# Two zero-padded q tiles per head, taken from a ring shared with the retention's states

## The chip, the cores and the metric

The kernel runs on one core of a Trainium2 chip. The metric is the device time of one execution in microseconds (us). TensorE (PE) does the matrix products and the transposes, VectorE (DVE) and ScalarE (ACT) work on their results, GpSimd (POOL) splits weights and copies small tiles, and the queue of SyncE (SP) issues most of the transfers. Each engine works through its own list of instructions in order. An instruction that waits for another engine also holds up everything behind it in its own list.

## What is computed

Two layers of a decoder over 1024 positions of width 1024. The part that matters here is layer 0's group A (8 heads of 64, each query keeps its 256 best keys) and layer 1's group C (4 heads with two softmax maps each). Both form scores block by block, 128 queries at a time against all keys up to the block:

```python
def causal_attention(q, k, v, scale):
    ...
    def block(args):
        qb, i = args
        qpos = i * QBLK + jnp.arange(QBLK)
        s = jnp.einsum('bqhd,bkhd->bhqk', qb, k).astype(jnp.float32) * scale
        s = jnp.where((kpos[None, :] <= qpos[:, None])[None, None], s, -jnp.inf)
        p = jax.nn.softmax(s, axis=-1).astype(v.dtype)
        return jnp.einsum('bhqk,bkhd->bqhd', p, v)
```

Group A does the same with a mask of the kept keys. Group B of layer 0 is a retention: a state per head is carried from chunk to chunk, `state = g * state + k'v`. Group D of layer 1 is a latent attention, which the change does not touch.

## The kernel before

Products in full precision are made from values split in two: a high part, and a low part that holds the remainder. For a pair of heads of A, `qs[r]` (r = 0, 1) holds the head's high q in 64 partitions and its low q in the other 64. The scores of one block are therefore two products into `S` (function `scores`): `qs` with `kd` (the high keys twice, line 411), and the high q with `kl` (the low keys, line 412). For the second product the other half of the partitions must read zeros. So POOL copies the block's high q into a tile of 128x128 whose other half was zeroed at the start: `zq[r]`, one tile for each r, filled by `head_q` (line 417) and read by line 412. There are 192 such products, 96 in A and 96 in C, fed by 64 copies each.

Order. A heads' pair is a list of units. A unit of A takes one r and two neighbouring blocks q = 2j and 2j + 1, with j in the order 0, 3, 1, 2; so the two blocks of a unit use the same `zq[r]` one right after the other. A unit of C takes one block and both r. A pipeline (`pipe.run`) lets each unit's scores go ahead of the transposes (`tp`, line 309) of the unit before, and mixes in the projections of the next pair as filling. What stands where in each engine's list is decided when the program is built, by priorities and free buffers; the copies of `head_q` carry a high priority. On POOL the copies share the list with the splits of weights (line 251, `waqkl`, `wagl`, `wavl`, `wol`) and with those of the mixed rows (`mixl`).

Softmax: DVE reads `S`, adds the mask and takes the extreme (line 1024), ACT takes the exponential (line 1026), DVE scales the row (line 973). PE transposes the result into `tp`, from which DVE (line 995) or ACT (line 993) copies it to `pT`; `tp` has two buffers. The product with v goes to `bank`, is multiplied with the gate `gin` on DVE (line 1013) and stored by SP to `mixT` (line 1014).

Rings. `med` is a ring of 5 tiles of 1 KB per partition. From it come the retention's masked scores `bsT` and its states `bstate` (which use half of a tile), the gates `gin`, `dl` (line 1085), and the angles `ang` and `kk` of a rope table (lines 223 to 232, on DVE). Head pairs are named here pair 0 to pair 3.

Of the kernel before, what the change touches and what calls it, by code (L numbers as in the profile page):

```python
# [11 lines left out]
F32 = mybir.dt.float32  # L12
F32R = mybir.dt.float32r
# [8 lines left out]
P = 128  # L22
# [67 lines left out]
def chain(*gens):  # L90
    for g in gens:
        yield from g
# [53 lines left out]
def tile_hybrid_decoder(ctx: ExitStack, tc, x, positions, pre_norm, post_norm, w_in_even, w_out_even, w_in_odd,  # L146
# [4 lines left out]
    const = ctx.enter_context(tc.tile_pool(name="const", bufs=1))  # L151
# [5 lines left out]
    sm = ctx.enter_context(tc.tile_pool(name="sm", bufs=4))  # L157
# [4 lines left out]
    def nm(s):  # L162
        n_[0] += 1
        return f"{s}_{n_[0]}"
# [7 lines left out]
    def epg(s, shape=(P, T), dt=F32):  # L172
        return ep.tile(list(shape), dt, tag="e", name=nm(s))
# [5 lines left out]
        return sm.tile(list(shape), dt, tag=s, name=nm(s), bufs=bufs)  # L179

    def med(s, shape=(P, 256)):
        return sm.tile(list(shape), F32, tag="med", name=nm(s), bufs=5)

    def hf(s, shape=(P, 512)):
        return sm.tile(list(shape), F32, tag="hf", name=nm(s), bufs=2)
# [4 lines left out]
    V, A, G = nc.vector, nc.scalar, nc.gpsimd  # L190
# [20 lines left out]

    halfpi = const.tile([P, 1], F32, name="halfpi")
    V.memset(halfpi, math.pi / 2)

    zq = [const.tile([P, P], F32R, name=f"zq{r}") for r in range(2)]
    for r in range(2):
        V.memset(zq[r][64 - r * 64:128 - r * 64, :].bitcast(F32), 0.0)

    def rope_tables(half, at, tabs, pg=epg):

# [182 lines left out]
    def scores(S, qs, kd, kl, q, qz=None):  # L403
# [5 lines left out]
        for c in range(0, n, 512):  # L409
            w = min(512, n - c)  # L410
            nc.tensor.matmul(S[:, c:c + w], a, kd[:, c:c + w], start=True, stop=False)  # L411
            nc.tensor.matmul(S[:, c:c + w], b, kl[:, c:c + w], start=False, stop=True)  # L412

    def head_q(qs, r, q):

        hp = slice(r * 64, r * 64 + 64)
        G.tensor_copy(zq[r][hp, :], qs[hp, q * P:q * P + P])  # L417
        return zq[r]


    vec = epg("vec", (P, P))
# [164 lines left out]
    def emit_mask(q):  # L586

        need, thr = tk["need"], tk["thr"]
        c = col[q]
        n = (q + 1) * P  # L590
        th = thr[:, c:c + 1]
        eq = epg("eq")
        cum = epg("cum")
        V.tensor_scalar(cum[:, 0:n], yt[q], th, None, op0=ALU.is_gt, op1=ALU.add, accum_out=need[:, c:c + 1])

        V.tensor_scalar(need[:, c:c + 1], need[:, c:c + 1], -1.0, float(TOPK), op0=ALU.mult, op1=ALU.add)
        yield 1
        V.tensor_scalar(eq[:, 0:n], yt[q], th, None, op0=ALU.is_equal)
        yield 1
        V.tensor_tensor_scan(cum[:, 0:n], eq[:, 0:n], eq[:, 0:n], 0.0, op0=ALU.add, op1=ALU.bypass)  # L600
        yield 1
        V.scalar_tensor_tensor(eq[:, 0:n], cum[:, 0:n], need[:, c:c + 1], eq[:, 0:n], op0=ALU.is_le, op1=ALU.mult)
        yield 1
        V.scalar_tensor_tensor(cum[:, 0:n], yt[q], th, eq[:, 0:n], op0=ALU.is_gt, op1=ALU.add)
        yield 1
        V.tensor_scalar(masks[q], cum[:, 0:n], 1.0, -NEG, op0=ALU.subtract, op1=ALU.mult)
        yield 1
# [44 lines left out]
    def retention(p):  # L652
# [45 lines left out]
        r = [pg2("br", (P, 4, 256)) for _ in range(2)]  # L698
# [26 lines left out]
        for n in range(NB):  # L725
            tsl = slice(n * P, n * P + P)
            kz, v = qk[n // 4][:, n % 4, P:256], vv[n // 4][:, n % 4, :]
            nxt = None
            if n < NB - 1:
                nxt = inner(n + 1)  # L730
                pu = pst("bu", "t")
                for h in range(2):
                    hp, hs = slice(h * 64, h * 64 + 64), slice(h * P, (h + 1) * P)
                    nc.tensor.matmul(pu[hp, 0:P], kz[:, hp], v[:, hs], start=True, stop=True)
            for _ in range(4):
                next(fill, 0)
            po = pst("bo", "s", (P, 2, 512))
            for h in range(2):
                hp, hs = slice(h * 64, h * 64 + 64), slice(h * P, (h + 1) * P)
                nc.tensor.matmul(po[:, h, 0:P], sT[:, hs], v[:, hs], start=True, stop=(n == 0))  # L740
                if n > 0:
                    nc.tensor.matmul(po[:, h, 0:P], qx[hp, tsl], state[hp, :], start=False, stop=True)
            sT = nxt
            if n < NB - 1:
                new = med("bstate")[:, 0:P]
                if state is None:
                    A.copy(new, pu[:, 0:P])
                else:
                    V.scalar_tensor_tensor(new, state, cs[:, C_G + p:C_G + p + 1], pu[:, 0:P], op0=ALU.mult, op1=ALU.add)
                state = new  # L750
            rr = r[n // 4][:, n % 4, :]
            V.tensor_copy(rr.rearrange("p (h t) -> p h t", t=P), po[:, :, 0:P])
            st6 = small("bst", (P, 2, 6))
            for h in range(2):
                V.bn_stats(st6[:, h, :], rr[:, h * P:(h + 1) * P])
                V.bn_aggr(mv[:, n * 2 + h, :], st6[:, h, :])
            if n % 4 == 3:

                hs = slice(n * 2 - 6, n * 2 + 2)
                V.tensor_scalar(rs[:, hs], mv[:, hs, 1], 4.0, 4.0 * EPS, op0=ALU.mult, op1=ALU.add)  # L760
                rsqrt_of(rs[:, hs], rs[:, hs])
            yield 1
# [274 lines left out]
        return pair_units(p, front, Aval[p], p * P, p * P, [ptg, ptg, ptg, pg2])  # L1037

    emit_threshold()
    todo = chain(*(emit_mask(q) for q in (6, 7, 4, 5, 2, 3)))  # L1040
    for i, _ in enumerate(chain(A_v(0), A_gate(0), A_qk(0))):
        if i % 4 == 3 and i >= 12:
# [432 lines left out]
```

## Time and profile before

| | |
|---|---|
| three runs | 1302.02, 1304.21, 1307.22 us, median 1304.21 |
| the profiled execution | 1303.41 us, of which the span of its instructions is 1301.6 us |
| granted TensorE clock, mean | 0.989 of full speed |
| busy: PE, DVE, ACT, POOL | 1246.0, 800.5, 682.6, 411.5 us |
| group A (attention of layer 0) | about 313 to 597 us of the span |
| group C | about 727 to 1041 us |

The page lists for each group of instructions its busy time and, behind a bar, how long its engine sat idle just before it and for whom. A granted clock of 1.00 is TensorE's level of 2.4 GHz, 0.50 the level of 1.2 GHz.

### The profile page before, as it was taken

How to read it: one execution, taken by the hardware profiler on the slowest of the kernel's cores; microseconds unless marked ns; L12 is line 12 of the kernel's file. 1: busy time of each engine (PE TensorE's matmuls, PEld its weight loads, DVE VectorE, ACT ScalarE, POOL GpSimd, SP SyncE). 2: the span in 40 equal slices, each digit the busy share in tenths (PEclk: the TensorE clock that was granted, in tenths of full speed). 3: DMA queues.
4: the chain of work that ended last, by engine and by line, in shares of the span. 5: the costliest groups of instructions: out<-in, count | busy, mean ns of one | idle time of the engine just before them, and what ended most of it. 6: DMA issues, size and time to landing. Idle time of an engine off the chain costs nothing.

```text
span 1301.6 us, 20092 instructions
## 1 busy us (share of the span) xinstructions
PE 1246.0 (96%) x7138; PEld 1029.2 (79%) x7138; DVE 800.5 (62%) x2020; ACT 682.6 (52%) x1510; POOL 411.5 (32%) x626
## 2 busy tenths in 40 slices
PE   7999989999999999889999999999999899999998
PEld 4788778798779877667887888889888777777786
DVE  6499999994654436484433344533654888887522
ACT  5578759602532424454545454554655677776421
POOL 4302232245251241444331233212322520435330
PEclk9999999999999999899999999999999999999999
DMA  5201111114121131225441113121322420232531
GB/s 192 57 25 34 33 34 57 34 26 121 29 71 32 34 89 40 79 89 184 148 121 42 49 49 90 58 60 42 122 65 89 110 53 30 75 97 66 187 125 65
DMA packets 92052, 97.70 MB, mean 75 GB/s; under 512 B 8118, under 2 KB 74448, under 8 KB 91952
## 3 DMA queue, kind: packets, MB, share of 16 engines
q1 hardware_dynamic: 87696, 82.39, 20.8%
q0 software_dynamic: 3968, 12.99, 3.6%
q8 instruction: 56, 0.92, 0.3%
q10 hardware_dynamic: 288, 1.05, 0.2%
q14 instruction: 44, 0.36, 0.1%
HBM read 68.74 MB, written 24.77 MB: 72 GB/s over the span
## 4 chain that ended last, share of the span: by engine, by line
PE 75%; DVE 13%; issue 4%; ACT 4%; POOL 4%; DMA 0%; POOLq 0%; DVEq 0%; ACTq 0%
PE tp L309 6%; PE bank L1009 5%; PE So L847 4%; PE So L848 4%; PE So L849 4%; DVE tj L519 3%; PE S L412 3%; PE S L411 3%; PE co L1176 2%; PE S L1419 1%; PE pav L301 1%; PE pav L303 1%; PE pav L302 1%; PE S L1421 1%; PE S L1420 1%
## 5 line engine op out<-in xcount | busy, mean ns | idle before, releaser
L1026 ACT ACTIVATE ae<-ae,nmx 128x128 f32<-128x128 f32 (+7 forms) x128 | 99.2, 776 | 90.1 <-DVE nmx L1024 89.6
L516 ACT ACTIVATE aj<-keys,tk_cand 128x1024 bf16<-128x1024 int16 (+5 forms) x96 | 93.2, 971 | 37.9 <-DVE tk_cand L537 14.9
L309 PE MATMUL tp<-cs,ae 128*128 128x128 f32 x576 | 89.3, 284 | 5.4 <-DVE pT L995 3.7
L309 PEld LDWEIGHTS tp<-cs,ae 128*128 128x128 f32 x576 | 68.7, 144 | 28.3 <-issue 9.3
L847 PE MATMUL So<-woh,mixl 128*128 128x512 f32 x224 | 87.7, 391 | 0.0
L849 PE MATMUL So<-woh,mixh 128*128 128x512 f32 x224 | 87.5, 391 | 0.0
L848 PE MATMUL So<-wol,mixh 128*128 128x512 f32 x224 | 87.5, 390 | 0.0
L1024 DVE CUSTOM_DVE_ANT_0 ce<-S,cmask 128x128 f32<-128x128 f32 (+7 forms) x64 | 48.2, 754 | 54.2 <-PE S L412 53.6
L519 DVE TENSOR_SCALAR_CACHE_REDUCE tj<-keys,tk_cand 128x384 bf16<-128x384 int16 (+5 forms) x96 | 79.9, 833 | 1.3
L1026 ACT ACTIVATE ce<-ce,nmx 128x128 f32<-128x128 f32 (+7 forms) x64 | 49.7, 776 | 53.0 <-DVE nmx L1024 52.7
L993 ACT COPY pT<-tp 128x384 f32<-128x384 f32 (+1 forms) x80 | 43.0, 538 | 54.4 <-PE tp L309 47.7
L995 DVE COPY pT<-tp 128x512 f32<-128x512 f32 (+1 forms) x80 | 50.7, 633 | 25.7 <-PE tp L309 22.8
L417 POOL CAST zq<-cqs 64x128 fp32r<-64x128 f32 x64 | 19.4, 304 | 146.9 <-PE S L412 143.3
L417 POOL CAST zq<-aqs 64x128 fp32r<-64x128 f32 x64 | 20.2, 316 | 129.7 <-PE S L412 127.1
L973 DVE TENSOR_SCALAR ae<-ae,ars 128x128 f32<-128x128 f32 (+7 forms) x96 | 58.4, 609 | 2.2
L1024 DVE CUSTOM_DVE_ANT_0 ae<-S,cmask,nrq 128x128 f32<-128x128 f32 (+3 forms) x64 | 51.4, 812 | 10.1 <-PE S L1421 8.3
L251 POOL TENSOR_TENSOR mixl<-mixr,mixh 128x512 fp32r<-128x512 f32 x32 | 41.5, 1306 | 35.3 <-ACT mixh L248 33.6
L412 PE MATMUL S<-akl,zq 128*128 128x512 f32 (+2 forms) x96 | 34.0, 365 | 17.2 <-POOL zq L417 17.2
L847 PEld LDWEIGHTS So<-woh,mixl 128*128 128x128 f32 x224 | 42.1, 188 | 9.3 <-issue 0.8
L848 PEld LDWEIGHTS So<-wol,mixh 128*128 128x128 f32 x224 | 42.1, 188 | 8.6
L849 PEld LDWEIGHTS So<-woh,mixh 128*128 128x128 f32 x224 | 42.1, 188 | 8.5
L329 ACT ACTIVATE junk<-So 128x512 bf16<-128x512 f32 x24 | 14.2, 593 | 56.0 <-PE So L849 42.2
(427 smaller groups left out, 4067.9 us busy)
## 6 DMA issues: line engine op xcount, KB each, us to landing
mixr<-mixT SPq DMA_DIRECT2D x32, 256.0 KB, 3.2
gT<-gate SPq DMA_DIRECT2D x24, 256.0 KB, 2.1
waqkr<-in_w_in_even_dram SPq DMA_DIRECT2D x32, 128.0 KB, 2.5
gin<-gT SPq DMA_DIRECT2D x32, 128.0 KB, 2.4
mixT<-gin SPq DMA_DIRECT2D x32, 128.0 KB, 1.8
wor<-in_w_out_even_dram SPq DMA_DIRECT2D x8, 512.0 KB, 4.0
xr<-in_x_dram POOLq DMA_DIRECT2D x8, 512.0 KB, 3.9
x1d<-xr SPq DMA_DIRECT2D x8, 512.0 KB, 3.3
```

Of the source, the lines that this page charges most:

```text
L309: nc.tensor.transpose(dst[:, k * P:(k + 1) * P], s, ident)
L412: nc.tensor.matmul(S[:, c:c + w], b, kl[:, c:c + w], start=False, stop=True)
L516: A.activation(aj[:, 0:n], src, AF.Sign, scale=-1.0, bias=edge, accum_out=dst)
L519: V.tensor_scalar(aj[:, 0:n], src, edge, None, op0=ALU.is_lt, op1=ALU.add, accum_out=dst)
L847: nc.tensor.matmul(dst, ml[k][:, bs], hi, start=(k == 0), stop=False)
L848: nc.tensor.matmul(dst, mh[k][:, bs], lo, start=False, stop=False)
L849: nc.tensor.matmul(dst, mh[k][:, bs], hi, start=False, stop=(k == kc - 1))
L973: V.tensor_scalar(e, e, rs, None, op0=ALU.mult)
L995: V.tensor_copy(pts[m][:, r, 0:n], tp[:, 0:n])
L1009: nc.tensor.matmul(bank[hp, o:o + wd], vp[:, kb, hp], pT[:, h, c:c + wd], start=(n == 0 or j == 0 and n == 1), stop=(n == len(jobs) - 1 or ...
L1024: V.tensor_tensor_reduce(out=e[:, 0:n], in0=S[:, 0:n], in1=mask, scale=scale, scalar=3.4e38, op0=ALU.add, op1=ALU.min, accum_out=nmx)
L1026: A.activation(e[:, 0:n], e[:, 0:n], AF.Exp, scale=-1.0, bias=nmx, accum_out=rsum)
```

## The change

`zq` becomes four tiles, one for each r and each parity of the block: `zq[r, q % 2]`. Even and odd blocks use them in turn. The tiles come from a new ring `quarter` of four tiles of 0.5 KB, from which the retention's states come first; for that `med` shrinks from 5 tiles to 4, so that the memory is the same. The four zero fills stand after the threshold search, no longer two at the start, and wait until the states that had the tiles are done with.

```diff
     def med(s, shape=(P, 256)):
-        return sm.tile(list(shape), F32, tag="med", name=nm(s), bufs=5)
+        return sm.tile(list(shape), F32, tag="med", name=nm(s), bufs=4)
+
+    def quarter(s, dt=F32):
+        return sm.tile([P, P], dt, tag="quarter", name=nm(s), bufs=4)
...
-    zq = [const.tile([P, P], F32R, name=f"zq{r}") for r in range(2)]
-    for r in range(2):
-        V.memset(zq[r][64 - r * 64:128 - r * 64, :].bitcast(F32), 0.0)
...
+    zq = {}
+
+    def new_zq():
+
+        for r in range(2):
+            for i in range(2):
+                zq[r, i] = quarter("zq", F32R)
+                V.memset(zq[r, i][64 - r * 64:128 - r * 64, :].bitcast(F32), 0.0)
+
     def head_q(qs, r, q):
 
         hp = slice(r * 64, r * 64 + 64)
-        G.tensor_copy(zq[r][hp, :], qs[hp, q * P:q * P + P])
-        return zq[r]
+        z = zq[r, q % 2]
+        G.tensor_copy(z[hp, :], qs[hp, q * P:q * P + P])
+        return z
...
-                new = med("bstate")[:, 0:P]
+                new = quarter("bstate")
...
     emit_threshold()
+    new_zq()
```

Three places show what this does to the order. The first is POOL's list where pair 3 begins: `wol` are splits of the output weights, `aqs_774/775` are q of pair 2, `aqs_861/862` q of pair 3 for r = 0 and 1. Before:

```order
L251 TENSOR_TENSOR mixl_989_5754<-mixr_987_5751,mixh_988_5753 128x512
L417 COPY zq0_113<-aqs_774_4675 64x128
L417 COPY zq0_113<-aqs_861_5133 64x128
L251 TENSOR_TENSOR mixl_992_5760<-mixr_990_5757,mixh_991_5759 128x512
L417 COPY zq1_114<-aqs_775_4676 64x128
L417 COPY zq1_114<-aqs_862_5134 64x128
L251 TENSOR_TENSOR wol_976_5728<-wor_977_5729,woh_975_5727 128x1024
L251 TENSOR_TENSOR wol_979_5734<-wor_980_5735,woh_978_5733 128x1024
L251 TENSOR_TENSOR mixl_1114_6227<-mixr_1112_6224,mixh_1113_6226 128x512
L251 TENSOR_TENSOR wol_982_5740<-wor_983_5741,woh_981_5739 128x1024
L251 TENSOR_TENSOR wol_985_5746<-wor_986_5747,woh_984_5745 128x1024
L417 COPY zq0_113<-aqs_861_5133 64x128 x2
```

After (line numbers are 9 higher for the copies, 1 lower for the splits; the tiles 509 and 510 belong to r = 0, 511 and 512 to r = 1):

```order
L250 TENSOR_TENSOR mixl_993_5758<-mixr_991_5755,mixh_992_5757 128x512
L426 COPY zq_509_3058<-aqs_865_5137 64x128
L426 COPY zq_510_3060<-aqs_865_5137 64x128
L250 TENSOR_TENSOR mixl_996_5764<-mixr_994_5761,mixh_995_5763 128x512
L426 COPY zq_511_3062<-aqs_866_5138 64x128
L426 COPY zq_512_3064<-aqs_866_5138 64x128
L250 TENSOR_TENSOR wol_980_5732<-wor_981_5733,woh_979_5731 128x1024
L250 TENSOR_TENSOR wol_983_5738<-wor_984_5739,woh_982_5737 128x1024
L250 TENSOR_TENSOR mixl_1118_6231<-mixr_1116_6228,mixh_1117_6230 128x512
L250 TENSOR_TENSOR wol_986_5744<-wor_987_5745,woh_985_5743 128x1024
L250 TENSOR_TENSOR wol_989_5750<-wor_990_5751,woh_988_5749 128x1024
```

Before, the copy for pair 3's second block (q = 1, r = 0) stands behind the four `wol`; after, the copies for q = 0 and q = 1 of both r stand ahead of them, and the next ones behind are for q = 6 and 7. The splits keep their places. It is the same all along: in the list after, nearly each place of a copy in A holds the copy that came next for its r before.

The second place is DVE's list at the same blocks. The rows of before are the same there, under other numbers; after, from the first score of pair 3 to the copies of the transposes that PE makes meanwhile for pair 2:

```order
L1033 ISA ae_971_5695,nmx_973_5700<-S_972_5696,cmask_87 128x128
L1033 ISA nmx_973_5700 128x1
L632 SCALAR_TENSOR_TENSOR gate_969_5690<-gate_969_5690,pag_964_5652 128x512
L978 RECIPROCAL ars_970_5694<-ars_970_5694 128x1
L1033 ISA ae_971_5695,nmx_975_5709<-S_974_5705,cmask_87 128x256
L1033 ISA nmx_975_5709 128x1
L982 TENSOR_SCALAR ae_971_5695<-ae_971_5695,ars_970_5694 128x128
L1004 COPY pT_962_5646<-tp_976_5714 128x512
L978 RECIPROCAL ars_970_5694<-ars_970_5694 128x1
```

Nothing moved here: the scaling of q = 0 (line 973 of before) stands ahead of the first copy of `pT`.

The third place is DVE's list near the end of pair 3, with the rope angles `ang`, `kk` and the small scalar `nlam`. Before:

```order
L223 TENSOR_TENSOR ang_1588_8655<-vT_383,cs_81 128x128
L973 TENSOR_SCALAR ae_1039_5968<-ae_1039_5968,ars_1029_5922 128x512
L225 TENSOR_SCALAR kk_1589_8656<-ang_1588_8655 128x128
L226 TENSOR_SCALAR kk_1589_8656<-kk_1589_8656 128x128
L1092 TENSOR_TENSOR nlam_6909<-dls_6903 128x1
L231 SCALAR_TENSOR_TENSOR ang_1588_8655<-kk_1589_8656,ang_1588_8655 128x128
L1013 TENSOR_TENSOR gin_1059_6034<-bank_1058_6017,gin_1059_6034 128x256
L1093 TENSOR_SCALAR nlam_6909<-nlam_6909 128x1
L231 SCALAR_TENSOR_TENSOR ang_1588_8655<-kk_1589_8656,ang_1588_8655 128x128 x2
L995 COPY pT_1063_6049<-tp_1062_6045 128x384
```

After:

```order
L222 TENSOR_TENSOR ang_1592_8659<-vT_379,cs_81 128x128
L982 TENSOR_SCALAR ae_1043_5972<-ae_1043_5972,ars_1033_5926 128x512
L1102 TENSOR_TENSOR nlam_6913<-dls_6907 128x1
L1103 TENSOR_SCALAR nlam_6913<-nlam_6913 128x1
L1022 TENSOR_TENSOR gin_1063_6038<-bank_1062_6021,gin_1063_6038 128x256
L1004 COPY pT_1067_6053<-tp_1066_6049 128x384
L1033 ISA ae_1069_6059,nmx_1071_6066<-S_1070_6060,mB_508_3057 128x640
L224 TENSOR_SCALAR kk_1593_8660<-ang_1592_8659 128x128
L225 TENSOR_SCALAR kk_1593_8660<-kk_1593_8660 128x128
```

The two `kk` and the `ang` behind them moved from ahead of `gin` and `pT` to behind them; with a ring of four, `kk` gets its tile only when the `gin` above it has been stored.

## Rows read from the trace of the kernel before

**Rows 1.** The page: busy time, share of the span, instructions.
```profile
PE 1246.0 (96%) x7138; PEld 1029.2 (79%) x7138; DVE 800.5 (62%) x2020; ACT 682.6 (52%) x1510; POOL 411.5 (32%) x626
```
**Rows 2.** PE's waits, 300 to 640 us: total us, times, longest.
```profile
PE S L412 <- POOL zq L417: 17.2, 6, 5.9
PE tp L309 <- DVE pT L995: 2.9, 1, 2.9
```
**Rows 3.** Groups by line: busy, mean ns | idle before.
```profile
L412 PE MATMUL S<-ckl,zq 128*128 128x512 f32 (+3 forms) x96 | 31.9, 346 | 0.0
```
**Rows 4.** Timeline of PE, five of the six waits: start, us, [idle before].
```profile
331.76 0.39 PE L412 MATMUL S<-akl,zq 128*128 128x256 f32 x1 [2.56 <-POOL zq L417]
...
390.69 0.39 PE L412 MATMUL S<-akl,zq 128*128 128x256 f32 x1 [3.15 <-POOL zq L417]
...
477.00 0.53 PE L412 MATMUL S<-akl,zq 128*128 128x256 f32 x1 [2.55 <-POOL zq L417]
...
545.19 0.58 PE L412 MATMUL S<-akl,zq 128*128 128x256 f32 x1 [5.95 <-POOL zq L417]
...
578.09 0.50 PE L412 MATMUL S<-akl,zq 128*128 128x512 f32 x1 [2.44 <-POOL zq L417]
```
**Rows 5.** Timeline of POOL before the first, second and fourth of these.
```profile
331.41 0.29 POOL L417 CAST zq<-aqs 64x128 fp32r<-64x128 f32 x1
...
385.56 1.42 POOL L251 TENSOR_TENSOR wavl<-wavr,wavh 128x256 fp32r<-128x256 f32 x2
...
534.32 4.77 POOL L251 TENSOR_TENSOR wol<-wor,woh 128x1024 fp32r<-128x1024 f32 x2 [5.17 <-ACT woh L248]
...
540.28 4.63 POOL L251 TENSOR_TENSOR wol<-wor,woh 128x1024 fp32r<-128x1024 f32 x2
544.85 0.28 POOL L417 CAST zq<-aqs 64x128 fp32r<-64x128 f32 x1
```
**Rows 6.** Timeline of PE: first products of q = 6, pairs 0 and 3.
```profile
335.60 0.40 PE L412 MATMUL S<-akl,zq 128*128 128x512 f32 x1
...
553.87 0.39 PE L412 MATMUL S<-akl,zq 128*128 128x512 f32 x1
```
**Rows 7.** Stretches: us, busy of PE, PEld, DVE, ACT, POOL, then clock, DMA.
```profile
391.75:395.16 3.41, 3.41 (x19) 3.41 (x18) 1.12 (x3) 0.44 (x3) 0.00 (x0) 0.50 0.40 120
477.08:480.50 3.42, 3.42 (x13) 3.02 (x14) 1.75 (x6) 0.98 (x3) 0.29 (x1) 0.50 0.63 197
541.94:548.76 6.82, 3.57 (x15) 3.29 (x15) 1.75 (x6) 1.08 (x3) 3.48 (x4) 0.50 0.19 60
579.48:586.31 6.83, 4.11 (x12) 3.11 (x12) 6.57 (x19) 3.00 (x7) 1.16 (x2) 0.50 0.06 19
```
**Rows 8.** Timeline of DVE, end of pair 3.
```profile
568.07 0.48 DVE L973 TENSOR_SCALAR ae<-ae,ars 128x512 f32<-128x512 f32 x1
...
571.23 1.83 DVE L223 TENSOR_TENSOR ang<-vT,cs 128x128 f32<-128x128 f32 x1
572.99 2.62 DVE L973 TENSOR_SCALAR ae<-ae,ars 128x512 f32<-128x512 f32 x1
...
577.92 2.51 DVE L226 TENSOR_SCALAR kk<-kk 128x128 f32<-128x128 f32 x1
...
581.60 0.55 DVE L995 COPY pT<-tp 128x384 f32<-128x384 f32 x1
```
**Rows 9.** Timeline of POOL in the same stretch.
```profile
570.54 7.26 POOL L251 TENSOR_TENSOR wol<-wor,woh 128x1024 fp32r<-128x1024 f32 x3 [0.17 <-POOL zq L417]
...
578.00 2.34 POOL L251 TENSOR_TENSOR wol<-wor,woh 128x1024 fp32r<-128x1024 f32 x1
```
**Rows 10.** The instructions of the zero fill: ns min/median/max, first and last start.
```profile
L217 DVE MEMSET zq<- x2: 165/165/165, 1.5 to 1.7; 64x128 f32 x2
```
**Rows 11.** Waits of SP's queue: total us, times, longest.
```profile
SPq L1014 <- DVE gin L1013: 211.2, 25, 24.1
```
**Rows 12.** The page, DMA issues: count, KB each, us to landing.
```profile
mixT<-gin SPq DMA_DIRECT2D x32, 128.0 KB, 1.8
```

## Prediction

> **What bounds the kernel now.** I read the busy table first: PE is busy for 1246.0 of 1301.6 us [rows 1], so the end moves almost only with PE, by what PE does or by its idle 55 us. Then the list of PE's waits in the stretch of group A. Nearly all of its idle time there has one cause: 17.2 us in six waits of line 412 for POOL's copy into `zq`, and 2.9 us in one wait for `pT` [rows 2]. In group C the same line waits for nothing [rows 3]. So the most that can come back directly is 17.2 us, all in A.
>
> Then the six places. Four are the second block (128x256) of a unit, three of them where a pair begins [rows 4]; the sixth wait, not shown, is what is left of the sum, 17.2 - 16.65 = 0.56 us. POOL's own rows tell why: the copy comes directly behind a run of splits, with no idle time of its own. At the first it starts at 331.41, at the fourth at 544.85, right behind four `wol` [rows 5]. PE had stood since 545.19 - 5.95 = 539.24. The copy itself takes 0.28 us; it is late because it had to wait for the product of the block before, and was therefore listed behind the splits.
>
> Last, the clock. Four stretches in A have a granted clock of 0.50, the level of 1.2 GHz, and each begins during or directly behind such a wait [rows 7]. In them PE was busy 3.41, 3.42, 3.57 and 4.11 us; work done at half the clock would have taken half, so they cost 1.7, 1.7, 1.8 and 2.1 us beyond the idle time.
>
> **The change part by part.**
>
> *The copies move ahead.* The copy for an odd block no longer waits for the even block's product, so it stands ahead of the splits. The place behind the splits goes to the copies for q = 6 and 7. Would PE now wait for those? At pair 0 the copy there ends at 331.41 + 0.29 = 331.70; PE needs it at 335.60 [rows 6], less the 2.56 us saved: 333.04, so 1.3 us are left. At pair 3 it ends at 545.13 and PE needs it at 553.87; less the gain there of 3.5 us, and not more than half of the last stretch, that is some 549. No new wait. The first, second and third waits and the small one come back in full: 2.56 + 3.15 + 2.55 + 0.56 = 8.82 us. The second and third also lose their slow stretch: 1.7 + 1.7 = 3.4 us. The first had none.
>
> *The fourth wait, 5.95 us, is not gained in full.* Behind the product PE transposes for pair 2 and makes one product of the output (some 1.8 us by the same work after the wait), up to 541.0; then it needs a `tp` buffer that DVE must first copy to `pT`. In DVE's list, in which nothing moved here, the scaling of q = 0 (line 973) stands ahead of that copy. What such a scaling does beside a `wol` the rows near the end of A show: 2.62 us for 128x512 while POOL runs `wol`, 0.48 us for the same shape without [rows 8, 9]; it ends just behind the end of a `wol`. Here it would start at some 540.6, just after the third `wol` (540.28), which ends at 540.28 + 2.3 = 542.6. With 0.3 us for itself and 0.6 for `pT`, PE goes on at 543.5 instead of standing from 539.24 to 545.19: it waits 2.45 us, and gains 3.5. Bounds: 0 if the scaling waits for the fourth `wol` too, 5.95 if not at all. The slow stretch may stay, since PE still idles about as long as at the first wait, which had none, and the third, which had one; I count nothing for it (bounds 0 and 1.8).
>
> The Trainium skill has a rule for this (SBUF — State Buffer, Who interferes with whom): a VectorE instruction with two SBUF inputs, or in a mode that uses two ports, and a GpSimd instruction that reads SBUF exclude each other for the whole instruction. The 2.62 us above agree with it. It speaks against a full gain: without it the fourth wait would bring 5.95 us and the sum below would be 2.45 us larger.
>
> *The sixth, 2.44 us, and the wait for `pT` behind it, 2.9 us.* After, the four `wol` come in one run (each 7.26 / 3 = 2.42 us [rows 9]), about 570.5 to 580.2. `ang`, the scaling and `nlam` stand ahead of `gin` and `pT`. `ang` and the scaling each end with a `wol`, as they do now [rows 8]; the first `nlam`, with two inputs in SBUF, probably ends with the third, at 577.8. The second `nlam` has one element a partition; if it isn't held, `gin` and `pT` take 1.0 us and PE goes on at 579.0 instead of 582.15 (the end of `pT` now, 581.60 + 0.55): 3.2 us gained. If it is held until 580.2, PE goes on at 581.3: 0.9. I take the middle, 2.0. Bounds: 0, because `kk` now stands behind this `gin` and waits for its store, which takes 1.8 us to land [rows 12], and holds the next scores on DVE; and 2.44 + 2.94 + 2.1 = 7.5 if nothing is late.
>
> *What is added.* Two more zero fills of 0.165 us [rows 10], now on DVE's list between the masks: 0.3 us at most, as DVE's own chain is on the path there in part. They wait for the last reads of the states. The third and fourth stand behind the copies of the retention's results that need the same products, so they hold nobody. The rings of four for the retention hold more of each kind than the shared ring of five did: nothing. The copies in C are one block earlier and were not waited for: nothing. On SP the load of a gate now stands behind a store in four places and waits some 1.8 us for it to land [rows 12]; I count nothing for it, and the last rival has the bound.
>
> **Sum:** 8.82 + 3.4 + 3.5 + 2.0 - 0.3 = 17.4 us. The profiled execution took 1303.41 us: 1286.0. The median of the three runs is 0.8 us above it: **1286.8 us**.
>
> **The rivals.**
>
> *All comes back* (every wait, all four slow stretches): 17.2 + 1.7 + 1.7 + 1.8 + 2.1 = 24.5 us, 1279.7. For it: PE has other work listed behind each of the six products. Against it: the order of DVE at the fourth and sixth places.
>
> *DVE takes POOL's place everywhere.* The scalings of the first two blocks are held in all the units where a pair begins, so the second and third waits return half with one slow stretch, and the fourth and sixth nothing: 2.56 + 1.6 + 1.3 + 0.56 + 1.7 = 7.7 us, 1296.5. Against it: the splits at pairs 1 and 2 are short pieces, 0.71 us each (1.42 for two [rows 5]), not 2.4.
>
> *Nothing moves:* the wait goes to the copies now behind the splits, or PE meets the same POOL through the split weights. 1302 to 1304. Against it: the 1.3 us and more left above.
>
> *Slower: SP stands at a gate.* With four `gin` tiles the load for a later product waits on SP until an earlier product has been made and stored, and the weight loads behind it wait too. One such wait for DVE's `gin` is up to 24.1 us long now [rows 11]. If one of them came onto PE's path in full: 1286.8 + 24.1 = 1311. It decides as soon as the loads are later than the splits' lead over their use; for the last `wol` of the fourth place that lead is about 9 us (544.91 to 553.87). Against it: these weight loads stood behind the same stores before; new is only the landing.
>
> **How the numbers follow.** Forecast 1286.8: 0.50. All back: 0.21. DVE in POOL's place: 0.17. Nothing: 0.08. Slower: 0.04. The range for 8 in 10 takes in the first two and the third: 1279 to 1297. A measurement of this kernel can tell about 0.5% from no change, 6.5 us, so faster means below 1297.7. That holds for the forecast, for all back and for most of the third: 0.86. Same takes the fourth case and the rest of the third: 0.10. Slower 0.04.
>
> **What would show it.** In the profile after, PE's waits for `zq` in A should be gone. At the fourth place PE should wait some 2.5 us for `pT`, with a line 973 of about 2 us ahead of it on DVE; near the end of A, `nlam` should be long and `pT` late. The slow stretches behind the second and third waits should be gone. It is wrong if line 412 still waits, if PE waits for split weights, or if PE's idle time falls and the span does not.

## The result and the profile after

| | before | after |
|---|---|---|
| median of the runs | 1305.51 us (1302.02 to 1307.22) | 1286.01 us (1285.33 to 1286.50) |
| ratio, 95% interval | | 0.985 (0.983 to 0.988) |
| profiled execution, its span | 1303.41, 1301.6 us | 1286.50, 1284.7 us |

The median before has one more run in it (1306.81 us) than the 1304.21 us from which the forecast was made.

The forecast was 1286.8 us. The busy table of after, which answers to [rows 1]:

```profile
PE 1243.6 (97%) x7138; PEld 1027.3 (80%) x7138; DVE 803.9 (63%) x2022; ACT 682.7 (53%) x1510; POOL 409.2 (32%) x626
```

PE does the same work and the span is 16.9 us shorter: PE lost idle time, and a little busy time that had been slow. PE's waits of after in A, 300 to 600 us, which answer to [rows 2] (line numbers as in the second order fence: 410 and 411 are 411 and 412 of before, 308 is 309, 1018 is 1009, 1033 is 1024, 1004 is 995, 1002 is 993, 982 is 973):

```profile
PE S L410 <- DVE nmx L1033: 3.2, 1, 3.2
PE tp L308 <- ACT pT L1002: 1.8, 2, 1.3
PE bank L1018 <- DVE pT L1004: 1.5, 2, 1.2
PE tp L308 <- DVE ae L982: 0.5, 1, 0.5
PE bank L1018 <- DVE akl L400: 0.2, 1, 0.2
```

No wait for `zq` is left. In its place stand DVE (5.4 us) and ACT (1.8 us). To see where the 16.9 us came from I cut both spans at the starts of PE's first `zq` product of pair 0, 1, 2, 3, of the first q = 6 of pair 3, and of group C. The columns are: stretch, its length, busy time (and instructions) of PE, PEld, DVE, ACT and POOL, then the granted clock, the DMA share and GB/s. Before:

```profile
328.51:386.61 58.10, 55.53 (x315) 44.72 (x314) 36.16 (x86) 27.93 (x58) 19.10 (x49) 1.00 0.16 43
386.61:473.77 87.16, 83.71 (x543) 72.61 (x541) 37.39 (x88) 29.43 (x64) 27.77 (x65) 0.98 0.17 46
473.77:538.57 64.80, 61.22 (x350) 48.38 (x349) 37.30 (x88) 32.44 (x63) 17.54 (x37) 0.97 0.23 74
538.57:553.87 15.30, 9.35 (x55) 7.13 (x54) 5.31 (x20) 3.66 (x11) 7.43 (x8) 0.78 0.13 44
553.87:727.25 173.38, 167.28 (x836) 133.74 (x835) 82.81 (x161) 87.27 (x171) 63.17 (x80) 0.98 0.36 112
```

After:

```profile
331.30:387.04 55.74, 55.22 (x316) 44.68 (x314) 36.73 (x86) 27.94 (x58) 18.97 (x49) 1.00 0.17 46
387.04:469.20 82.16, 81.89 (x542) 70.98 (x541) 37.82 (x88) 29.37 (x64) 27.93 (x65) 1.00 0.18 49
469.20:528.83 59.63, 59.16 (x351) 47.08 (x349) 37.75 (x88) 32.38 (x63) 17.50 (x37) 1.00 0.25 80
528.83:537.98 9.15, 7.63 (x55) 5.33 (x53) 8.34 (x20) 3.56 (x11) 7.44 (x8) 1.00 0.19 59
537.98:711.23 173.25, 167.94 (x836) 134.23 (x835) 80.32 (x161) 87.20 (x171) 62.89 (x80) 0.98 0.36 113
```

Pairs 0 to 2 are now full: PE is busy for all but 0.3 to 0.5 us of each stretch. The fourth stretch, around the fourth wait, shrank from 15.30 to 9.15 us, and its clock is 1.00 and not 0.78. The fifth, with the end of A, gained almost nothing.

**The fourth place** went as the prediction drew it. DVE, then the `wol` of POOL beside it, then PE, of after:

```profile
530.60 2.36 DVE L982 TENSOR_SCALAR ae<-ae,ars 128x128 f32<-128x128 f32 x1
532.89 0.68 DVE L1004 COPY pT<-tp 128x512 f32<-128x512 f32 x1
...
533.67 1.68 DVE L982 TENSOR_SCALAR ae<-ae,ars 128x256 f32<-128x256 f32 x1
535.27 0.55 DVE L1004 COPY pT<-tp 128x384 f32<-128x384 f32 x1
...
530.51 4.68 POOL L250 TENSOR_TENSOR wol<-wor,woh 128x1024 fp32r<-128x1024 f32 x2
...
533.62 1.94 PE L1018 MATMUL bank<-pT,av 128*64 128x256 f32 x16 [1.21 <-DVE pT L1004]
535.87 0.86 PE L1018 MATMUL bank<-pT,av 128*64 128x128 f32 x6 [0.31 <-DVE pT L1004]
```

The first scaling, of the smallest shape, takes 2.36 us and ends near the end of one `wol` (530.51 + 2.34); the second takes 1.68 us and ends with the other (535.2). The same shapes take 0.29 us (at 536.78) and 0.36 us (at 537.27) when POOL has no split. The copies from `tp` to `pT` are not held: the one at 532.89 takes 0.68 us beside the second `wol`. PE waits 1.5 us in all.

**The end of A** is where a new wait stands. POOL, DVE and PE there:

```profile
554.57 4.72 POOL L250 TENSOR_TENSOR wol<-wor,woh 128x1024 fp32r<-128x1024 f32 x2 [0.17 <-POOL zq L426]
561.01 4.68 POOL L250 TENSOR_TENSOR wol<-wor,woh 128x1024 fp32r<-128x1024 f32 x2 [1.72 <-ACT woh L247]
...
556.98 2.53 DVE L1098 TENSOR_TENSOR dl<-dl 128x64 f32<-128x64 f32 x2 [2.52 <-DMA dl<-in_diff_lambda_dram]
...
563.05 0.42 DVE L224 TENSOR_SCALAR kk<-ang 128x128 f32<-128x128 f32 x1 [0.72 <-DMA mixT<-gin]
563.51 2.27 DVE L225 TENSOR_SCALAR kk<-kk 128x128 f32<-128x128 f32 x1
...
566.02 0.95 DVE L1033 CUSTOM_DVE_ANT_0 ae<-S,mB 128x768 f32<-128x768 f32 x1
...
567.04 0.79 PE L410 MATMUL S<-akd,aqs 128*128 128x512 f32 x1 [3.24 <-DVE nmx L1033]
```

`kk` waits for the store of `gin`, then its second step is held until the last `wol` ends (565.7). Only then does DVE read the score block that PE needs free, and PE stands for 3.24 us. The clock falls to half near the end of this wait, from 566.51 on, for 6.83 us.

### The profile page after: what moved, and what is told of

Same layout as the page of the kernel before. It is cut to its first block, busy times and chain, and to the rows that moved or that the text cites. A ratio compares the mean times of both kernels' runs of the same rounds, so it can differ in the third digit from the quotient of the medians.

```text
span 1284.7 us, 20092 instructions
## 1 busy us (share of the span) xinstructions
PE 1243.6 (97%) x7138; PEld 1027.3 (80%) x7138; DVE 803.9 (63%) x2022; ACT 682.7 (53%) x1510; POOL 409.2 (32%) x626
## 4 chain that ended last, share of the span: by engine, by line
PE 77%; DVE 14%; ACT 3%; issue 3%; DMA 1%; POOL 1%; SPq 0%; POOLq 0%; DVEq 0%; ACTq 0%
PE tp L308 5%; PE bank L1018 5%; PE So L856 4%; PE So L857 4%; PE So L858 4%; DVE tj L528 3%; PE S L410 3%; PE S L411 3%; PE co L1186 2%; PE S L1429 1%; PE pav L300 1%; PE pav L302 1%; PE pav L301 1%; PE S L1431 1%; PE S L1430 1%
## 5 line engine op out<-in xcount | busy, mean ns | idle before, releaser
L308 PE MATMUL tp<-cs,ae 128*128 128x128 f32 x576 | 86.1, 277 | 4.4 <-ACT pT L1002 3.0
L982 DVE TENSOR_SCALAR ae<-ae,ars 128x128 f32<-128x128 f32 (+7 forms) x96 | 61.1, 639 | 2.1
L250 POOL TENSOR_TENSOR wol<-wor,woh 128x512 fp32r<-128x512 f32 (+1 forms) x24 | 39.2, 1652 | 7.3 <-ACT woh L247 6.9
```

Of the source, the lines that this page charges most:

```text
L250: (eng or V).tensor_tensor(lo, src, hi.bitcast(F32), op=ALU.subtract)
L308: nc.tensor.transpose(dst[:, k * P:(k + 1) * P], s, ident)
L982: V.tensor_scalar(e, e, rs, None, op0=ALU.mult)
```

## Experiments

All kernels are the changed kernel with an edit, unless said otherwise. The ratio is to the kernel before as it ran beside each (its medians there lie between 1303.56 and 1306.86 us), with an interval of some 0.002 to either side. So a difference of 2 to 4 us between two medians from different sets of runs is not shown by them alone; there the reading rests on the traces. The columns from "A starts" on divide the span as above, in one profiled execution of each kernel; "A starts" is when A's first `zq` product starts.

| kernel | median | ratio | A starts | pair 0 | pair 1 | pair 2 | pair 3 to q = 6 | to C | C to end |
|---|---|---|---|---|---|---|---|---|---|
| before | 1305.51 | 1 | 328.51 | 58.10 | 87.16 | 64.80 | 15.30 | 173.38 | 574.35 |
| after | 1286.01 | 0.985 | 331.30 | 55.74 | 82.16 | 59.63 | 9.15 | 173.25 | 573.47 |
| e1 one tile per r | 1305.79 | 1.001 | 331.26 | 59.35 | 87.21 | 64.94 | 15.21 | 171.65 | 574.58 |
| e2 in turn in pair 3 alone | 1297.66 | 0.994 | 330.72 | 59.43 | 87.14 | 64.92 | 9.16 | 171.53 | 573.70 |
| e3 rope table in C | 1283.74 | 0.983 | 328.08 | 55.71 | 82.15 | 59.61 | 9.18 | 168.36 | 575.91 |
| e4 scaling on ACT | 1282.10 | 0.982 | 330.89 | 55.01 | 82.17 | 59.67 | 7.16 | 170.87 | 573.93 |
| e5 splits in pieces | 1281.87 | 0.983 | 331.94 | 55.71 | 82.18 | 59.59 | 8.49 | 169.18 | 573.91 |
| e6 tiles without ring | 1282.99 | 0.984 | 328.88 | 55.78 | 82.24 | 59.61 | 9.18 | 170.76 | 574.35 |
| e7 splits on DVE | 1279.02 | 0.980 | 331.31 | 55.71 | 82.19 | 59.62 | 7.50 | 167.02 | 574.05 |
| e8 e4 and e3 together | 1279.83 | 0.981 | 330.65 | 55.01 | 82.18 | 59.63 | 7.16 | 170.23 | 575.74 |
| e9 before, splits on DVE | 1290.35 | 0.988 | 329.26 | 59.46 | 85.57 | 63.26 | 8.92 | 165.76 | 574.47 |
| e10 e7 and e4 together | 1277.76 | 0.978 | 331.40 | 54.99 | 82.17 | 59.62 | 8.16 | 167.07 | 573.59 |
| e11 before again | 1306.26 | - | 329.50 | 59.43 | 87.16 | 64.86 | 15.41 | 173.39 | 574.75 |
| e12 e10, two fills more | 1277.58 | 0.978 | 331.12 | 55.02 | 82.18 | 59.61 | 8.01 | 166.72 | 573.14 |

**Is it the tiles or the rings?** e1 undoes the tiles alone.

```diff
-        z = zq[r, q % 2]
+        z = zq[r, 0]
```

> The changed kernel with one thing undone: even and odd blocks use the same tile of their r; the ring of quarters, the shorter ring of med and the four zero fills stay. Theory (the tiles carry the gain): the six waits of the second product for POOL's copy are back, 15 to 20 us in A, with slow stretches behind the second to fourth, and the time is that of the kernel before, 1302 to 1307 us. Rival (the rings carry it, or a part): 1286 to 1296 us.

1305.79 us, ratio to before 1.001 (0.9996 to 1.0023). PE's wait of e1 in A:

```profile
PE S L411 <- POOL zq L426: 18.9, 7, 5.9
```

So the gain is the tiles': without their alternation the rings and fills bring nothing. e6 takes the other half away: the tiles as constants, the states in `med` again.

```diff
-                zq[r, i] = quarter("zq", F32R)
+                zq[r, i] = const.tile([P, P], F32R, name=f"zq{r}{i}")
...
-                new = quarter("bstate")
+                new = med("bstate")[:, 0:P]
```

> The changed kernel with the four tiles as constants instead of a ring, and the retention's states in the ring of med again, which has four tiles; the memory is the same. Theory (the rings cost and bring nothing before A; states and masked scores get along in four tiles): group A and the time as in the changed kernel, 1284 to 1288 us. Rival (the states need the room): PE waits in the retention for bsT or states, 2 us or more there, 1288 to 1295 us.

1282.99 us: the rival falls, and the time is below the expected range: in its trace A starts 2.4 us earlier than in after, and the half-clock stretch near the end of A is missing. The memory is the same, so the shared ring was not needed; by the ratios (0.984 and 0.985) it is not shown that the ring costs time.

**Does each place gain for itself?** e2 uses the tiles in turn in pair 3 alone.

```diff
-    def head_q(qs, r, q):
+    def head_q(qs, r, q, alt=True):
...
-        z = zq[r, q % 2]
+        z = zq[r, q % 2 if alt else 0]
...
-                qz = head_q(qs[r], r, q)
+                qz = head_q(qs[r], r, q, p == 3)
```

> The changed kernel, but the two tiles are used in turn for pair 3 alone; pairs 0 to 2 use one tile per r (group C still uses two). Theory (each place gains for itself): the waits at pairs 0 to 2 are back and cost 12 to 13 us against the changed kernel, 1298 to 1300 us; from the first score of pair 3 to its first product of q = 6 it takes 9 us as in the changed kernel, not 15. Rival (pair 3 gained only because POOL and DVE came there earlier): that stretch takes 12 us or more and the time is 1301 to 1306 us.

1297.66 us, just under the range. Pairs 0 to 2 take what they take in e1, the stretch at pair 3 what it takes in after (9.16 us). What pair 3 gains does not hang on the pairs before it, so the terms can be read one by one.

**What makes DVE late at pair 3?** Three edits ask in different ways. e4 takes the scalings of the first two blocks off DVE:

```diff
-                    if merge and (qq + r) % 2 == 0:
+                    if merge and (qq + r) % 2 == 0 or not merge and j == 0:
                         A.activation(e, e, AF.Copy, scale=rs)
```

> The changed kernel, but the scalings of the first two blocks of a head of A (line 982 for 128x128 and 128x256) are made by ACT instead of DVE. Theory (at the start of pair 3 the copy to pT is late because a scaling ahead of it on DVE is held by a split on POOL): PE's waits there, 1.5 us, fall to 0.3 us or less; 1 to 2 us less than the changed kernel, 1284 to 1285 us. Rival (PE waits there for something else, or ACT's added work makes the exponentials late): the waits stay at 1 us or more, 1286 to 1290 us.

1282.10 us, better than expected. The stretch at pair 3 falls by 2.0 us to 7.16. DVE and PE there in e4 (the copy to `pT` comes directly behind the extreme, and the product `bank` waits for nothing):

```profile
529.52 0.69 DVE L1004 COPY pT<-tp 128x512 f32<-128x512 f32 x1
...
530.24 0.55 PE L308 MATMUL tp<-cs,ae 128*128 128x128 f32 x3 [0.31 <-ACT pT L1002]
...
531.06 2.60 PE L1018 MATMUL bank<-pT,av 128*64 128x256 f32 x24
```

Another 0.7 us comes at pair 0 and 2.4 us behind pair 3, where PE waits as long as in after (3.25 us) but the clock stays up; that these 2.4 us come from the edit is not shown. e5 leaves everything where it is and cuts POOL's splits into four:

```diff
-                    split_hl(hi, lo, raw, eng=G, hi_eng=self.hi_eng)
+                    A.copy(hi, raw)
+                    for c in range(0, 1024, 256):
+                        G.tensor_tensor(lo[:, c:c + 256], raw[:, c:c + 256], hi[:, c:c + 256].bitcast(F32), op=ALU.subtract)
```

> The changed kernel, but POOL makes each low part of an output weight of layer 0 that is split in group A in four pieces of 128x256 instead of one instruction of 128x1024. Theory (DVE's instructions that read and write SBUF stand until the split instruction that is running ends): at the start of pair 3 the first scaling (128x128) falls from 2.36 us to 1 us or less, since it stands for one piece (some 0.6 us) at most, and PE's waits for pT there from 1.5 us to 0.5 us or less; near the end of pair 3 no instruction of DVE of this kind is over 1.2 us; 3 to 5 us less than the changed kernel, 1281 to 1283 us. Rival (POOL keeps DVE out as long as it has splits to do, piece by piece): the same instructions still take 2 us or more, 1286 us.

1281.87 us, as expected. DVE's first two scalings (line 984 there), POOL's row and pieces beside them, and PE's one wait at this place:

```profile
531.20 0.90 DVE L984 TENSOR_SCALAR ae<-ae,ars 128x128 f32<-128x128 f32 x1
...
532.81 0.74 DVE L984 TENSOR_SCALAR ae<-ae,ars 128x256 f32<-128x256 f32 x1
...
530.73 1.30 POOL L250 TENSOR_TENSOR mixl<-mixr,mixh 128x512 fp32r<-128x512 f32 x1
531.98 5.65 POOL L831 TENSOR_TENSOR wol<-wor,woh 128x256 fp32r<-128x256 f32 x8
...
537.91 0.50 PE L411 MATMUL S<-akl,zq 128*128 128x512 f32 x1 [1.14 <-POOL zq L426]
```

The hold follows the length of POOL's instruction. The second scaling stands among the pieces (0.71 us each) and takes 0.74 us, not 1.68. The first takes 0.90 us, not 2.36, but what it stands beside is the end of `mixl` (at 532.03) and no piece, so it says nothing of the pieces. Eight pieces take 5.65 us where two whole splits took 4.68, however, so POOL is later with the copy for q = 6, and 1.14 us comes back as a wait for `zq`. The larger part of e5's gain is near the end of A: `kk` takes 0.35 and 0.65 us there, PE still waits 2.2 us for `nmx`, and no half-clock stretch follows. e7 takes the splits off POOL:

```diff
-                    split_hl(hi, lo, raw, eng=G, hi_eng=self.hi_eng)
+                    split_hl(hi, lo, raw, eng=V, hi_eng=self.hi_eng)
```

> The changed kernel, but DVE itself makes the low parts of the output weights of layer 0 in group A, so that no such split runs on POOL. Theory (the splits on POOL hold DVE's scalings, kk and dl): no instruction of line 982, 224, 225, 1098 or 1102 in the last two stretches is over 1.2 us long, PE's waits of 1.5 and 3.2 us are gone, and the time is 1281 to 1284 us, if DVE's eight added splits (some 1.1 us each by the rate of its 128x1024 work) fit into its idle time. Rival (they stand ahead of the first scores of pair 3 on DVE and PE waits there instead): 2 to 5 us of waits for nmx or pT at the start of pair 3, 1286 to 1291 us.

1279.02 us, better than expected. DVE's four splits at pair 3 take most of their time where DVE would be idle; the extreme of pair 3's first scores starts 1.2 us later than in after (530.31 and 529.14):

```profile
524.45 2.55 DVE L250 TENSOR_TENSOR wol<-wor,woh 128x1024 fp32r<-128x1024 f32 x2
527.24 3.14 DVE L250 TENSOR_TENSOR wol<-wor,woh 128x1024 fp32r<-128x1024 f32 x2 [0.24 <-ACT woh L247]
```

PE's two largest waits of A in e7:

```profile
PE tp L308 <- DVE pT L1004: 1.3, 1, 1.3
PE tp L308 <- ACT pT L1002: 1.1, 2, 0.6
```

No instruction of the named lines is over 0.75 us between pair 3's first product and C (the longest is a scaling of 128x1024), and `kk`, `dl` and `nlam` take 0.23, 0.23 and 0.15 us at most. The waits of 1.5 and 3.2 us are gone; the two above stand in their place. e5 shortens the split and the hold shortens with it, e7 takes the split off POOL and the hold is gone, e4 takes the held scaling off DVE and the wait for `pT` is gone. So it is shown that the splits on POOL hold DVE's scalings and `kk`; the same pattern stands for `dl` (2.4 us for the first of the two in after, 0.23 in e7) and `nlam` (only e3 has it held for a whole split, see below). The Trainium skill (SBUF — State Buffer, Who interferes with whom), on which the prediction drew, has the engine that comes second blocked for the whole instruction of the other. The traces agree: the holds end within 0.2 us of the end of one POOL instruction.

**The end of A.** e3 moves the rope table out of it.

```diff
-        rope_tables(16, C_INV16, tabD, med)
+        rope_tables(16, C_INV16, tabD)
```

> The changed kernel, but the angles and kk of the second rope table come from the ring of the score pages instead of med, which moves their instructions on DVE out of the end of pair 3 into group C; the lists of PE and POOL are the same. Theory (kk, behind the store of a gate and then held beside a split, keeps PE from the next scores): PE's wait of 3.2 us near the end of pair 3 and the half-clock stretch behind it are gone, 3 to 6 us less than the changed kernel, 1280 to 1283 us. Rival (the splits hold the scalings there anyway, or the tables cost the same in C): a wait of the same size for pT or nmx in the same 20 us, 1285 to 1288 us.

1283.74 us, above the range by 0.7. The wait of 3.2 us and the slow stretch are gone, and the stretch to C is 4.9 us shorter. In C 2.4 us are lost again against after: there DVE's table stands ahead of a gate, and a wait appears in C that after does not have:

```profile
PE plat L300 <- DVE gate L632: 1.1, 1, 1.1
```

So `kk` at the end of A costs 3.2 us by its wait and up to 2.5 us by the clock behind it. The profiled execution (1280.78 us) is the fastest of e3's four, with A 3.2 us earlier than in after; the median gains less than its trace. e8 puts e3 and e4 together.

> Both of two earlier edits together on the changed kernel: the scalings of the first two blocks on ACT, and the second rope table in C. Theory (they take away different waits, but both took away the one half-clock stretch near the end of pair 3): from the first score of A to the first score of C the two alone gained 5.0 and 4.9 us; together 2.0 + 0.7 at the start of the pairs, 2.3 to 2.7 for the one slow stretch and 3.2 for the wait, some 7.5 to 8 us, and 2 us are lost again in C: 1279 to 1282 us. Rival (the gains overlap wholly): 1282 to 1284 us.

1279.83 us, in the range, but not by the sum that was expected: from A's start to C it gains 5.7 us and not 7.5 to 8, since a wait for `pT` (ACT) that takes 1.43 us in e3 and 0.48 in e4 now takes 1.90, and a slow stretch of 3.41 us begins behind it, which neither has:

```profile
566.52 0.55 PE L308 MATMUL tp<-cs,ae 128*128 128x128 f32 x3 [1.90 <-ACT pT L1002]
```

In after PE does not wait at this place: with the wait of 3.2 us gone, another is uncovered. But the profiled execution (1282.43 us) is the slowest of e8's four, 2.6 us above the median, so the others need not have lost this much.

**Are the tiles still worth it without splits on POOL?** e9 is the kernel before with the edit of e7.

> The kernel before (one tile per r), but DVE makes the low parts of the output weights of layer 0 in group A, so that no such split runs on POOL. Theory (the waits at the start and the end of pair 3 come from these splits alone, those at pairs 0 to 2 from others): the waits of the second product for POOL fall from 17.2 us to 9 us, those of 5.95 and 2.44 us are gone; from the first score of pair 3 to its first product of q = 6 it takes 7.5 to 9 us, not 15.3; 1291 to 1295 us. Rival (the copy for the next block of the same r is late there anyway, because it must wait for the product of the block before): 1298 us or more.

1290.35 us, just under the range. PE's waits in A:

```profile
PE S L412 <- POOL zq L417: 10.0, 5, 3.2
```

This one edit brings 16.5 us (from the 1306.86 us of before beside it), most of what the change brings and by other means: of the fourth wait 1.09 us is left and the sixth is gone, with the splits that caused them. About 3 us of it is something else: the waits at pairs 1 and 2 are still there in full (3.16 and 2.58 us), but in this trace, the fastest of e9's four, no half-clock stretch follows them. Why is not shown. The tiles then still bring 9 to 11 us (9.3 between the traces, 11.3 between medians that were not taken side by side), mainly at pairs 0 to 2. e10 joins e7 and e4.

> The changed kernel with both edits that take DVE and POOL apart: the splits of the output weights in A on DVE, and the scalings of the first two blocks on ACT. Theory (with no split on POOL the scalings are not held any more, so moving them brings only what pair 0 gained, 0.7 us): 1277 to 1279 us, the same as with the splits on DVE alone. Rival (the scalings delay pT also without a split): 2 us less than that, 1276 us.

1277.76 us (ratio to before 0.978, 0.976 to 0.980), as expected and the fastest so far: 0.7 us at pair 0, and nothing more at pair 3 (8.16 us; 7.50 in e7).

**Why does A start later?** In the profiled executions A starts 2.8 us later after than before. e11 is the kernel before once more.

> The kernel before, unchanged, for a second trace. Theory (the start of A differs by some 3 us from one execution to the next, whatever the kernel, because DVE and POOL meet differently in the retention): the first score of A starts between 328 and 332 us, and from there to the first score of C it takes 398 to 399 us as in the first trace. Rival (the 2.8 us by which A starts later in the changed kernel belong to the change): it starts at 328.5 us within 0.3 us.

A starts at 329.50 us: the rival's 328.5 within 0.3 does not hold. The start lies in the theory's range, 1.0 us from the first trace; a spread of 3 us is not shown. From there to C it takes 400.25 us, not the expected 398 to 399 and 1.5 us more than in the first trace, nearly all of it at pair 0: there the same first wait (2.58 us, 2.56 in the first trace) has a half-clock stretch behind it, as in e1, e2 and e9. Only the first trace of before had none. e12 asks whether the later start hangs on DVE's list, which is two instructions shorter ahead of this place.

```diff
-    V.memset(halfpi, math.pi / 2)
+    _ = [V.memset(halfpi, math.pi / 2) for _ in range(3)]
```

> The kernel of the run before last (changed kernel, splits of the output weights in A on DVE, scalings of the first two blocks on ACT), and two more tiny fills at DVE's start (a 128x1 constant written three times), which put back the two instructions that DVE's list lost at its start with the two zero fills; nothing else moves. In all nine kernels with the ring DVE idles 0.26 to 0.28 us at one place before A (line 528, at about 105 us, waiting for nothing that the profile shows), in the four without it never, and these start A at 328.5 to 329.5 us, those at 330.7 to 331.9 (one at 328.1). Theory (the gap depends on how many instructions stand ahead in DVE's list): the gap at 105 us is gone or elsewhere, the line of the first product bqk starts 4.2 us behind the first split wbvl, not 4.9, A starts at 328 to 330 us, and the time is 1275 to 1277 us. Rival (the gap and the later start come from the ring itself): the gap stays, 4.9 us, A starts at 331 us, 1277 to 1279 us.

1277.58 us, the rival's time. DVE's row at the place in after, and in e12:

```profile
105.01 0.61 DVE L528 TENSOR_SCALAR_CACHE_REDUCE tj<-keys,tk_cand 128x384 bf16<-128x384 int16 x1 [0.28 <-issue]
```

```profile
105.33 0.60 DVE L528 TENSOR_SCALAR_CACHE_REDUCE tj<-keys,tk_cand 128x384 bf16<-128x384 int16 x1
```

The gap is gone, and `bqk` starts 4.2 us behind `wbvl` again and not 4.9: the gap does depend on how many instructions stand ahead (e6, whose four fills stand at the start, has none either). But A still starts at 331.12 us. Nine of ten kernels with the ring start A at 330.6 to 331.9 us, one (e3, with the same list as after up to there) at 328.1; the four without it at 328.5 to 329.5. Compared instruction by instruction, DVE of after, 0.2 us ahead up to 104 us, falls behind DVE of before in four steps, all before the fills at 269 us: 0.7 us at the gap, 0.6 at 118 to 130 us (behind a half-clock stretch of 6.83 us from 108.99 on that before lacks), 0.6 at about 207 us and 1.1 between 230 and 238 us. The last step is found between these two rows, in before, after and e11:

```profile
226.45 0.69 DVE L782 TENSOR_TENSOR rT<-btr,bg 128x512 f32<-128x512 f32 x1
238.73 0.42 DVE L752 COPY br<-bo 128x256 f32<-128x256 f32 x1
...
228.18 0.69 DVE L791 TENSOR_TENSOR rT<-btr,bg 128x512 f32<-128x512 f32 x1
241.52 0.42 DVE L761 COPY br<-bo 128x256 f32<-128x256 f32 x1
...
226.30 0.69 DVE L782 TENSOR_TENSOR rT<-btr,bg 128x512 f32<-128x512 f32 x1
239.67 0.42 DVE L752 COPY br<-bo 128x256 f32<-128x256 f32 x1
```

It is 12.28 us in before, 13.34 in after and 13.37 in e11, which is before itself. In between, steps of the search for the thresholds on three elements a partition take 0.5 to 0.8 us each beside POOL's splits and casts, not some 0.2, three of them in before and six in the other two. So DVE and POOL do meet differently from one execution to the next, as the theory of e11 said, and this step does not belong to the change. The step at 207 us is found in e6 too, which has no ring. Why nearly all kernels with the ring meet the late case stays open.

## Why the prediction was right

The time was right to 0.8 us. That it was so close is luck: two terms and one that was put at 0.3 us are off by 1.9 to 2.7 us each, and the errors cancel. Right in the mechanism are the copies and the fourth wait. Term by term, on the profiled executions:

| step of the prediction | forecast | measured |
|---|---|---|
| first wait (pair 0) | 2.56 | 2.36 |
| second wait and its slow stretch (pair 1) | 4.85 | 5.00 |
| third and small wait, slow stretch (pair 2) | 4.81 | 5.17 |
| fourth wait (pair 3 to q = 6) | 3.5 | 6.15 |
| sixth wait and the one for `pT` (to C) | 2.0 | 0.13 |
| added, and all ahead of A | -0.3 | -2.79 |
| C to the end | 0 | 0.88 |
| sum | 17.4 | 16.9 |

*The copies move ahead: right.* Waits one to three came back in full with the slow stretches, and e2 shows that they do so place by place. No new wait for the copies behind the splits arose in after; e5 shows how near it is, since longer splits on POOL made one of 1.14 us.

*The fourth wait: mechanism right, size off.* The scaling was held and PE waited for `pT`, but for 1.5 us and not 2.45. PE had more to do first (besides what I had counted, the second head's first scores and the start of `bank`, up to 532.4), so 4.4 us came back. And the slow stretch, which I counted at nothing, came back with its 1.8 us. Both were inside the bounds. A second scaling was held as well (1.68 us, beside the last `wol`), which the sum did not have; it cost PE 0.3 us.

*The sixth wait: the lower bound came true, and the path of the sum did not.* I took the middle, 2.0 us, between `nlam` held and not held, with the four `wol` in one run, and bounds 0 and 7.5. In after the `wol` come two and two (554.57 and 561.01): the first `dl` is held until the second `wol` ends, and ACT, which needs it, does the cast for the third `wol` only behind that:

```profile
559.80 0.20 ACT L1100 ACTIVATE dls<-dls 128x2 f32<-128x2 f32 x1 [3.71 <-DVE dls L1099]
559.91 1.03 ACT L247 CAST woh<-wor 128x1024 fp32r<-128x1024 f32 x1
```

`ang` (0.29 us), the scaling (0.48) and `nlam` (0.15) fall into the gap between the two runs and are not held. So `nlam` was not long, though the prediction had named that as a sign. The reason named for the bound 0 is what happened: `kk` behind `gin` waited for its store and held the next scores, 3.24 us, and a wait of 1.3 us for a `pT` of ACT stands ahead of it. The slow stretch behind it is not certain: e6, with a wait of 3.3 us at the same place, has none, and its stretch to C is 2.5 us shorter. That the order of DVE's list puts `kk` behind a store was known; its price could have been worked out, as a wait plus a held `kk` (2.5 us by [rows 8]), instead of being left to a bound.

*What was added: the sign was right, the size was not.* The four fills take 0.165 us each, at 269 to 277 us, and nobody waits for them. That A starts later was not foreseen; about 1.1 us of it is no part of the change (e11), and the rest is only partly explained. The 0.88 us behind the start of C have no cause on record.

*The clock.* I read from one trace that the first wait has no slow stretch. Four other traces have one there, worth 1.3 us. Before is 2.1 us slower on the median (1305.51) than in its profiled execution (1303.41), and the gain on the medians, 19.5 us, is larger than the 16.9 of the two traces. Such a stretch would account for 1.3 us of this; which of the runs of before had one is not on record.

*The rivals.* "All comes back" fails at the end of A, and at the fourth place for 1.5 us; "DVE takes POOL's place everywhere" is right on the sixth term, which it put at nothing, and at the fourth place for 1.5 us only; "nothing moves" and "slower" have no trace: no wait of PE for a gate or a weight load appeared in A.

## What to carry to other kernels

Here a second buffer for an operand gained what its waits cost, place by place, plus the half-clock work behind them, except where DVE was late then; read at each place what the waiting engine would do next, and who is late then. Where a long elementwise instruction on POOL overlaps DVE, it also delays short instructions of DVE that read and write SBUF (2.36 us for one of 0.29), so cut it, move it, or take DVE's short steps away; here moving eight splits from POOL to DVE was worth some 16 us without the second buffer (3 of them not shown to come from it) and 7 us with it. When a ring gets shorter, look at what its next user now stands behind: a store that nobody waited for can come onto the path.

## What was not expected of the hardware

The clock did not answer the same wait in the same way. Behind 2.56 us of waiting it stayed up in one execution of before, and behind 2.58 us it fell in another. Behind the waits of 3.2 and 2.6 us at pairs 1 and 2 it fell in before, e11, e1 and e2 and stayed up in e9. Behind the wait of 3.2 us near the end of A it fell in after and stayed up in e4. The stretches from near the end of that wait on, in after and in e4 (columns as above):

```profile
566.51:573.34 6.83, 6.30 (x25) 3.85 (x26) 4.88 (x16) 3.45 (x7) 0.00 (x0) 0.51 0.00 0
```

```profile
563.90:570.90 7.00, 6.48 (x42) 4.74 (x43) 6.00 (x18) 4.62 (x10) 0.00 (x0) 1.00 0.06 19
```

PE is busy nearly throughout in both, and gets 25 instructions done in one and 42 in the other. A single trace therefore tells what a slow stretch costs, but not whether a wait has one.

An instruction on one element a partition can be held as well: `nlam` took 2.36 us in e3, with a `wol` beside it, and 0.15 us in after.
